# Attention scores as 64-row matmuls, one per head, in place of one full-height matmul over zero-masked keys

## The chip, the core and the metric

The kernel runs on one NeuronCore of one Trainium2 chip. The metric is the device time of one execution in microseconds (us). The engines go by the names of the profile: PE is TensorE's matmul, PEld its weight load, DVE is VectorE, ACT ScalarE, POOL GpSimd, SP SyncE, whose queue issues nearly all DMAs.

## What is computed

One inference step of a four-part decoder trunk: attention, MLP, state-space mixer, MLP, for 512 prompt tokens and 8 sampled tokens. The change lies in the attention of the prompt. There are three groups of window and dilation, (128, 1), (512, 4) and (2048, 16), each with 16 heads of 64 features. Queries and keys are rotated (rope: the two halves of 32 features of a head are mixed by cos and sin), and each query attends to a band of keys:

```python
def dilated_band_attention(q, k, v, dil, nstep):       # q, k, v: (1, 512, 16, 64)
    qb, kx, vx = blocks(q), with_prev(blocks(k)), with_prev(blocks(v))
    scores = jnp.einsum('brnqhe,brnkhe->brnhqk', qb, kx) * SCALE
    scores = jnp.where(mask[None, None, :, None], scores, -jnp.inf)
    mx = jnp.max(scores, -1, keepdims=True)
    p = jnp.exp(scores - mx)
    den = jnp.sum(p, -1)
    o = jnp.einsum('brnhqk,brnkhe->brnqhe', p, vx) / jnp.swapaxes(den, -1, -2)[..., None]
    lse = jnp.swapaxes(mx[..., 0] + jnp.log(den), -1, -2)
```

The three groups' outputs are merged by a softmax over `lse`, and the keys and values of the last positions are outputs too.

## The kernel before

Activations lie features first: a tile of 128 partitions holds 128 features of all 520 tokens. A large product is made of three matmuls for each piece of 128 input features (high part of the weight by high and low part of the activation, low part of the weight by the high part), 24 in a row, for half of the tokens; `dense` issues them (line 249, output `psd`). The kernel is written as a sequence of **slots**. A slot issues one `dense`, then lets each of several **lanes** (generators that hold the small work) take a step, then hands on the weight pipeline (`feed`: `whi` on ACT, lines 186 and 190, and `wlo` on DVE, line 197), evacuates `psd`, and lets the lanes take another step. `after(n, f)` runs `f` at the start of the small work of the n-th next slot. Nothing reorders this afterwards: each engine runs its instructions in the order in which they were written.

The attention runs over 8 chunks `c` of 128 features, that is, of two heads, and in a chunk over the groups g = 0, 1, 2. A group has four slots of q and k (`project_qk`) and two of v (`project_v`); in the last chunk the v slots come after all others. The q and k weights are laid out so that one `psd` holds the first halves of both heads' q and k, and another the second halves. The rope on DVE (lines 575 to 587) gives the tiles F1 and F2. In the slot after, `gather` (lines 594 to 597) has ACT move quarters between partitions in three copies, so that F1 holds q and F2, renamed K, holds k, in rows of half, head, feature. One slot later `heads` (line 604) writes `Kz`: two copies of K, each multiplied by a column of zeros and ones that leaves one head's rows; for g = 1 and 2 it also brings the keys in the order of the dilation, by reading every fourth token.

`attn_scores` (lane A) transposes k for the cache (`kT`, `nT`), then makes the scores: at line 780 the queries of a block are the stationary operand and the keys of both heads in `Kz` the moving one, so that one matmul gives head 0's scores and head 1's scores beside each other in one PSUM bank. Group 0 has four such steps of one block each, groups 1 and 2 two steps of two blocks. After each step DVE adds the mask and takes the maximum (line 792, output `prob`), and ACT takes the exponentials (`exps`, line 807). When group 2 of a chunk is done, `attn_apply` (lane B) merges the groups' factors (`fac`), scales the probabilities (ACT line 846, DVE line 848), transposes them (`pT`, line 869; each bank of them is copied to SBUF by ACT and DVE in turn, lines 256 and 258) and multiplies by V (`oN`, `oR`, line 862, in tiles of 64 columns). `attn_sample` (lane C) does the 8 sampled tokens: `sT` (line 904) is transposed, `spr` (ACT, line 910) takes its exponential, DVE scales that (lines 913 and 914), and `sP` (line 920) transposes it back. `attn_values` transposes v (`vT`, line 666).

PSUM has eight banks: three for `psd`, three (tag S) shared by `kT`, `nT`, `s`, `sT`, `sP`, `pT`, `vT` and others, and two for `oN` and `oR`. A bank that is taken again waits until its last reader is done. The v slots' `psd` is evacuated by ACT (line 618), the q and k slots' by DVE.

Of the kernel before, what the change touches and what calls it, by code (L numbers as in the profile page):

```python
# [11 lines left out]
AF = mybir.ActivationFunctionType  # L12
# [5 lines left out]
P = 128  # L18
D = 1024
KD = D // P  # L20
SEQ = 512
NB = 8
NT = SEQ + NB
# [12 lines left out]
NDB, NSB, NVB = 3, 3, 2  # L36
# [43 lines left out]
class Net:  # L80
# [93 lines left out]
    def split_hi(self, s):  # L174
        nc = self.nc
        for _ in range(2 if s.kind == "qk" else 1):
            s.out.append((self.unit("whi", F32R)[:, 0:D], self.unit("wlo", F32R)[:, 0:D]))
        todo = []
        if s.kind == "qk":
            for ab in range(2):  # L180
                hi, lo = s.out[ab]
                for i, raw in enumerate(s.raw):
                    src = raw.rearrange("p (k h a e) -> p k h a e", k=KD, h=2, a=2)[:, :, :, ab, :]
                    dh = hi.rearrange("p (k i h e) -> p k i h e", k=KD, i=2, h=2)[:, :, i]
                    dl = lo.rearrange("p (k i h e) -> p k i h e", k=KD, i=2, h=2)[:, :, i]
                    nc.scalar.activation(out=dh, in_=src, func=AF.Copy)
                    todo.append((dl, src, dh))
        else:
            hi, lo = s.out[0]
            nc.scalar.activation(out=hi, in_=s.raw[0], func=AF.Copy)  # L190
            todo.append((lo, s.raw[0], hi))
        self.half_split = (s, todo)
# [368 lines left out]
    def project_qk(self, g, x, cur, sqk):  # L561

        nc = self.nc
        F1, F2 = self.pair("F")
        if g != 1:
            cur["K2"] = list(self.pair("K"))
        K = cur["K2"].pop(0)
        cur["F1"][g], cur["F2"][g] = F1, K
        m = {}

        def rope_a(half):
            def f(p1):
                c0 = half * HALF
                m[half] = self.unit("ropem").rearrange("p (i t) -> p i t", i=4)
                nc.vector.tensor_tensor(out=m[half][:, 0:2], in0=p1.unsqueeze(1).broadcast_to((P, 2, HALF)),  # L575
                                        in1=self.cossin[:, :, c0:c0 + HALF], op=ALU.mult)
            return f

        def rope_b(half):
            def f(p2):  # L580
                c0 = half * HALF
                cs = slice(c0, c0 + HALF)
                t = m[half]
                nc.vector.tensor_tensor(out=t[:, 2:4], in0=p2.unsqueeze(1).broadcast_to((P, 2, HALF)),
                                        in1=self.cossin[:, :, cs], op=ALU.mult)
                nc.vector.tensor_tensor(out=F1[:, cs], in0=t[:, 0], in1=t[:, 3], op=ALU.subtract)
                nc.vector.tensor_tensor(out=F2[:, cs], in0=t[:, 2], in1=t[:, 1], op=ALU.add)
                if half:
                    self.after(1, gather)
                    self.after(2, heads)  # L590
            return f

        def gather():
            lo, hi = slice(0, 64), slice(64, P)
            nc.scalar.activation(out=K[lo], in_=F1[hi], func=AF.Copy)
            nc.scalar.activation(out=K[hi], in_=F2[hi], func=AF.Copy)
            nc.scalar.activation(out=F1[hi], in_=F2[lo], func=AF.Copy)

        def heads():
            kz = self.unit("Kz")[:, 0:2 * SEQ].rearrange("p (h t) -> p h t", h=2)  # L600
            src = K[:, 0:SEQ] if g == 0 else K[:, 0:SEQ].rearrange("p (m r) -> p r m", r=4)
            for h in range(2):
                dst = kz[:, h] if g == 0 else kz[:, h].rearrange("p (r m) -> p r m", r=4)
                nc.scalar.activation(out=dst, in_=src, func=AF.Copy, scale=self.hmask[:, h:h + 1])
            cur["Kz"][g] = kz

        for half in range(2):
            self.slot(lambda: self.dense(self.weights(sqk, 0), x, half), rope_a(half))
            self.slot(lambda: self.dense(self.weights(sqk, 1), x, half), rope_b(half))
# [74 lines left out]
    def attn_scores(self, c, g, cur, o, late):  # L684

        nc = self.nc
        F1, F2 = cur["F1"][g], cur["F2"][g]
        kb = self.blocks(F2, g)
        out = self.O[2 + g][0, 0].rearrange("t k (c h) e -> t k c (h e)", h=2)[:, :, c, :]
        self.load_cache(c, g, 0, cur)  # L690
        if not late:
# [2 lines left out]
            yield  # L694
            yield
        bk = self.bank("S", "kT", NSB)
        natural = lambda t: t.rearrange("p (h a e) -> p a h e", h=2, a=2)
        ident = self.ident.rearrange("p (a h e) -> p a h e", a=2, h=2)
        for i in ((3,) if g == 0 else range(4)):
            nc.tensor.transpose(natural(bk[:, i * P:(i + 1) * P]), kb[i], ident)  # L700
        ts = [F1, F2] if late else [F1, F2, cur["V"][g]]
        bn = self.bank("S", "nT", NSB)
        for i, t in enumerate(ts):
            row = bn[0:NB, i * P:(i + 1) * P]
            if i < 2:
                nc.tensor.transpose(natural(row), t[:, SEQ:NT], ident)
            else:
                nc.tensor.transpose(row, t[:, SEQ:NT], self.ident)
        yield
        if g == 0:  # L710
            cur["scr"] = self.dp.tile([3, 3, NB, P], F32, name="newscr", tag="newscr", bufs=2)
# [46 lines left out]

        st = cur["st"]
        neg = self.sp.tile([P, 2, 4], F32, name="neg", tag="neg", bufs=2)  # L760
        kz = cur["Kz"][g]
        both = lambda t: t.rearrange("p (h k) -> p h k", h=2)
        pts = []
        for js in ((0,), (1,), (2,), (3,)) if g == 0 else ((0, 1), (2, 3)):
            if not pts:
                pts = list(self.pair("prob"))
            pt = pts.pop(0)
            b = self.bank("S", "s", NSB)
            tiles, q0 = [], 0
            for j in js:  # L770
                if g == 0:
                    n = P if j == 0 else 2 * P
                    k0 = max(j - 1, 0) * P
                    q, ks = F1[:, j * P:(j + 1) * P], slice(k0, k0 + n)
                    mask = self.m0[:, 2 * P - n:2 * P]
                else:
                    n = P
                    q, ks = F1[:, j:SEQ:4], slice(j * P, (j + 1) * P)
                    mask = self.m0[:, P:2 * P] if g == 1 else self.m2
                nc.tensor.matmul(both(b[:, q0:q0 + 2 * n]), q, kz[:, :, ks], start=True, stop=True)  # L780
                for h in range(2):
                    cs = slice(q0, q0 + n)
                    tiles.append((b[:, cs], pt[:, cs], mask, st[:, 1 if g else 0, j, h, g], neg[:, h, j:j + 1]))
                    for i in range(n // P):
                        key = j if g else j - (n // P - 1) + i
                        cur["P"][g, h, j, key] = pt[:, q0 + i * P:q0 + (i + 1) * P]
                    q0 += n
            a, j1 = 1 if g else 0, js[-1] + 1
            mx, ng = st[:, a, js[0]:j1, :, g, 0], neg[:, :, js[0]:j1].rearrange("p h j -> p j h")
            yield  # L790
            for sc, pr, mask, one, _ in tiles:
                nc.vector.tensor_tensor_reduce(out=pr, in0=sc, in1=mask, scale=1.0, scalar=NEG,  # L792
                                               op0=ALU.add, op1=ALU.max, accum_out=one[:, 0:1])
            nc.vector.tensor_scalar(out=ng, in0=mx, scalar1=-SCALE, scalar2=None, op0=ALU.mult)  # L794
            self.after(1, lambda tiles=tiles: self.exps(tiles))
            yield
# [838 lines left out]
```

## Time and profile before

| | |
|---|---|
| median of 3 runs | 1977.77 us (1975.17 to 1977.83) |
| profiled execution | 1976.72 us, of which 1974.9 us are the span of its instructions |
| PE busy | 1908.9 us, 97% of the span |
| PEld busy | 1853.0 us, 94% |
| DVE busy | 1289.4 us, 65% |
| ACT busy | 954.4 us, 48% |
| mean granted TensorE clock | 0.978 |

Busy times are unions: overlapping matmuls count once. The attention takes the first 660 us of the span. A row of a timeline gives the start and the length of an instruction or of a run of like ones; a matmul's length includes the time in which it fills and drains, so the pace of PE is read from one start to the next. A float32 matmul that isn't a transpose shows as two records, one for each of its two passes.

### The profile page before, as it was taken

To read this page: it belongs to the slowest core of one execution; us is meant where nothing else is said; L and a number is where in the kernel's file an instruction comes from. 1 tells how busy PE (TensorE), PEld (TensorE's weight loads), DVE (VectorE), ACT (ScalarE), POOL (GpSimd) and SP (SyncE) were. 2 spreads that over 40 slices of the span, in tenths; PEclk is the share of its full clock that TensorE was granted. 3 is DMA by queue.
4 is the path that set the end of the run, shared out by engine and by line. 5 is a ranking of instruction groups with operands and counts; after the bars stand their busy time and mean duration, and the time that the engine had idled before them with its cause. 6 is when DMAs were issued, how large, how long until landed. Compare 5 with 4: busy or idle time off the path is not lost.

```text
span 1974.9 us, 38305 instructions
## 1 busy us (share of the span) xinstructions
PE 1908.9 (97%) x15530; PEld 1853.0 (94%) x15530; DVE 1289.4 (65%) x2769; ACT 954.4 (48%) x2085; POOL 73.4 (4%) x92
## 2 busy tenths in 40 slices
PE   7999999999998899999999999998999899999997
PEld 7999999999997899999999999998999899999996
DVE  4676776776788753333337769987889786465435
ACT  4565664664674363525153556634555273525241
POOL 0010010010010000000000000000000000000002
PEclk9999999999998989999999999988999899999999
DMA  6665655555567327655554256644657569987411
GB/s 195 176 181 154 181 157 154 166 157 159 141 206 238 107 98 245 208 170 183 193 186 134 87 175 203 217 133 156 215 186 238 163 184 312 277 277 208 129 33 44
DMA packets 407833, 346.91 MB, mean 176 GB/s; under 512 B 17676, under 2 KB 392932, under 8 KB 405984
## 3 DMA queue, kind: packets, MB, share of 16 engines
q1 hardware_dynamic: 405608, 344.26, 56.3%
q8 instruction: 122, 2.00, 0.4%
q0 software_dynamic: 2048, 0.20, 0.2%
q14 instruction: 55, 0.45, 0.1%
HBM read 322.41 MB, written 130.99 MB: 230 GB/s over the span
## 4 chain that ended last, share of the span: by engine, by line
PE 80%; DVE 14%; ACT 3%; DMA 1%; issue 1%; SPq 0%; POOL 0%; DVEq 0%; ACTq 0%
PE psd L249 68%; PE s L780 3%; DVE wlo L197 2%; DVE conv L1088 2%; PE pT L869 1%; PE oR L862 1%; DVE acc L388 1%; PE oN L862 1%; PE so L945 1%; DVE conv L1216 1%; PE vT L666 1%; ACT ab L1288 1%; DVE ys L1390 1%; PE kT L700 1%; DVE x L392 1%
## 5 line engine op out<-in xcount | busy, mean ns | idle before, releaser
L249 PE MATMUL psd<-x,whi 128*128 128x260 f32 x5920 | 1120.5, 290 | 13.4 <-ACT x L390 5.8
L249 PEld LDWEIGHTS psd<-x,whi 128*128 128x128 f32 x5920 | 930.4, 191 | 33.7 <-issue 15.8
L249 PE MATMUL psd<-x,wlo 128*128 128x260 f32 x2960 | 842.6, 285 | 2.9 <-DVE wlo L197 2.9
L249 PEld LDWEIGHTS psd<-x,wlo 128*128 128x128 f32 x2960 | 563.8, 190 | 3.4 <-DVE wlo L197 3.4
L197 DVE TENSOR_TENSOR wlo<-wraw,whi 128x1024 fp32r<-128x1024 f32 (+1 forms) x321 | 334.2, 1060 | 60.9 <-ACT whi L190 32.3
L249 PE MATMUL psd<-hid,whi 128*128 128x260 f32 (+2 forms) x2048 | 369.8, 283 | 0.1
L190 ACT ACTIVATE whi<-wraw 128x1024 fp32r<-128x1024 f32 x225 | 234.0, 1049 | 211.7 <-PE psd L249 140.9
L249 PEld LDWEIGHTS psd<-hid,whi 128*128 128x128 f32 x2048 | 315.7, 188 | 0.3 <-DVE hid L541 0.3
L249 PE MATMUL psd<-hid,wlo 128*128 128x260 f32 (+2 forms) x1024 | 289.1, 282 | 0.0
L249 PEld LDWEIGHTS psd<-hid,wlo 128*128 128x128 f32 x1024 | 192.7, 188 | 0.0
L489 DVE TENSOR_TENSOR acc<-acc,psd 128x260 f32<-128x260 f32 (+2 forms) x160 | 67.6, 423 | 148.1 <-PE psd L249 148.0
L541 DVE TENSOR_TENSOR hid<-relu,hid 128x260 fp32r<-128x260 f32 x128 | 54.4, 428 | 165.2 <-ACT hid L538 165.2
L534 ACT ACTIVATE relu<-psd 128x260 f32<-128x260 f32 x128 | 49.4, 386 | 159.9 <-PE psd L249 159.1
L807 ACT ACTIVATE prob<-prob,neg 128x128 f32<-128x128 f32 (+1 forms) x192 | 79.5, 416 | 54.1 <-DVE neg L794 53.7
L249 PE MATMUL psd<-ypart,whi 128*128 128x260 f32 x512 | 101.6, 297 | 2.5 <-DVE ypart L1453 2.4
L249 PEld LDWEIGHTS psd<-ypart,whi 128*128 128x128 f32 x512 | 82.6, 197 | 4.2 <-DVE ypart L1453 3.0
L575 DVE TENSOR_TENSOR ropem<-psd,trig 128x520 f32<-128x520 f32 x48 | 33.4, 696 | 77.7 <-PE psd L249 77.6
L1088 DVE SCALAR_TENSOR_TENSOR conv<-raw,cvcols,conv 128x511 f32<-128x511 f32 (+2 forms) x96 | 71.9, 749 | 6.2 <-ACT conv L1083 4.0
L249 PE MATMUL psd<-ypart,wlo 128*128 128x260 f32 x256 | 74.3, 290 | 0.0
L780 PE MATMUL s<-Kz,F 128*128 128x256 f32 (+1 forms) x192 | 71.7, 483 | 0.0
L1170 ACT ACTIVATE raw<-psd 128x260 f32<-128x260 f32 x64 | 24.4, 382 | 84.0 <-PE psd L249 82.4
L792 DVE CUSTOM_DVE_ANT_0 prob<-s,cb 128x128 f32<-128x128 f32 (+1 forms) x192 | 51.6, 318 | 20.5 <-PE s L780 20.5
(252 smaller groups left out, 2277.3 us busy)
## 6 DMA issues: line engine op xcount, KB each, us to landing
wraw<-in_mlp_w_dram SPq DMA_DIRECT2D x128, 512.0 KB
wraw<-in_attn_w_in_dram SPq DMA_DIRECT2D x72, 512.0 KB
wraw<-in_ssm_w_in_dram SPq DMA_DIRECT2D x49, 512.0 KB
cache<-in_cache_kv_w_dram SPq DMA_DIRECT2D x32, 512.0 KB
state<-in_state_ssm_dram SPq DMA_DIRECT2D x32, 512.0 KB
out_dram<-in_cache_kv_w_dram SPq DMA_DIRECT2D x16, 1016.0 KB
qb<-newscr SPq DMA_DIRECT2D x16, 512.0 KB
ab<-acs SPq DMA_DIRECT2D x16, 512.0 KB
```

What stands on the lines that cost most here:

```text
L190: nc.scalar.activation(out=hi, in_=s.raw[0], func=AF.Copy)
L197: self.nc.vector.tensor_tensor(out=lo, in0=src, in1=hi.bitcast(F32), op=ALU.subtract)
L249: self.nc.tensor.matmul(out, a, b[:, cs], start=n == 0, stop=n == 3 * len(w) - 1)
L489: nc.vector.tensor_tensor(out=a, in0=a, in1=ps, op=ALU.add)
L534: nc.scalar.activation(out=t[:, 0], in_=ps, func=AF.Relu)
L541: nc.vector.tensor_tensor(out=h[m][1][:, cs], in0=t[:, 1], in1=h[m][0][:, cs].bitcast(F32), op=ALU.subtract)
L575: nc.vector.tensor_tensor(out=m[half][:, 0:2], in0=p1.unsqueeze(1).broadcast_to((P, 2, HALF)), in1=self.cossin[:, :, c0:c0 + HALF], op=ALU ...
L780: nc.tensor.matmul(both(b[:, q0:q0 + 2 * n]), q, kz[:, :, ks], start=True, stop=True)
L792: nc.vector.tensor_tensor_reduce(out=pr, in0=sc, in1=mask, scale=1.0, scalar=NEG, op0=ALU.add, op1=ALU.max, accum_out=one[:, 0:1])
L807: self.nc.scalar.activation(out=pr, in_=pr, func=AF.Exp, scale=SCALE, bias=ng, accum_out=st[:, 1:2])
L862: nc.tensor.matmul(bank[hs, j * P:(j + 1) * P], vt[:, hs], pr, start=first, stop=last)
L1088: nc.vector.scalar_tensor_tensor(out=t[:, j:SEQ], in0=raw[:, 0:SEQ - j], scalar=w[:, 3 - j:4 - j], in1=t[:, j:SEQ], op0=ALU.mult, op1=ALU.add)
```

## The change

The weights are laid out with the head outermost, so that F1 and F2 come out in rows of head, (q or k), feature. `gather` now makes K in rows of head, half, feature, in six copies of 32 partitions; for g = 1 and 2 it also brings the keys in the order of the dilation, so that each of the four K copies becomes one of 512 tokens, read with a step of four, and one of the 8 sampled tokens. `heads` and `Kz` are gone. The transposes for the cache need no permuted identity, and for g = 1 and 2 read k without a step. The scores are two matmuls, each with the 64 rows of one head as contraction, head 0 on partitions 0 to 63 and head 1 on 64 to 127, each into a bank of its own; group 0 has two steps of two blocks, groups 1 and 2 one step of four blocks.

```diff
         def gather():
-            lo, hi = slice(0, 64), slice(64, P)
-            nc.scalar.activation(out=K[lo], in_=F1[hi], func=AF.Copy)
-            nc.scalar.activation(out=K[hi], in_=F2[hi], func=AF.Copy)
-            nc.scalar.activation(out=F1[hi], in_=F2[lo], func=AF.Copy)
-
-        def heads():
-            kz = self.unit("Kz")[:, 0:2 * SEQ].rearrange("p (h t) -> p h t", h=2)
-            src = K[:, 0:SEQ] if g == 0 else K[:, 0:SEQ].rearrange("p (m r) -> p r m", r=4)
             for h in range(2):
-                dst = kz[:, h] if g == 0 else kz[:, h].rearrange("p (r m) -> p r m", r=4)
-                nc.scalar.activation(out=dst, in_=src, func=AF.Copy, scale=self.hmask[:, h:h + 1])
-            cur["Kz"][g] = kz
+                a, b = slice(64 * h, 64 * h + 32), slice(64 * h + 32, 64 * h + 64)
+                for d, s in ((a, F1[b]), (b, F2[b])):
+                    if g == 0:
+                        nc.scalar.activation(out=K[d], in_=s, func=AF.Copy)
+                    else:
+                        nc.scalar.activation(out=K[d, 0:SEQ].rearrange("p (r m) -> p r m", r=4),
+                                             in_=s[:, 0:SEQ].rearrange("p (m r) -> p r m", r=4), func=AF.Copy)
+                        nc.scalar.activation(out=K[d, SEQ:NT], in_=s[:, SEQ:NT], func=AF.Copy)
+                nc.scalar.activation(out=F1[b], in_=F2[a], func=AF.Copy)
...
-        for js in ((0,), (1,), (2,), (3,)) if g == 0 else ((0, 1), (2, 3)):
...
-            b = self.bank("S", "s", NSB)
+        for js in ((0, 1), (2, 3)) if g == 0 else (range(4),):
+            pts = self.pair("prob")
+            bs = [self.bank("S", "s", NSB) for _ in range(2)]
...
-                nc.tensor.matmul(both(b[:, q0:q0 + 2 * n]), q, kz[:, :, ks], start=True, stop=True)
+                cs = slice(q0, q0 + n)
                 for h in range(2):
-                    cs = slice(q0, q0 + n)
+                    hs, b, pt = slice(64 * h, 64 * h + 64), bs[h], pts[h]
+                    nc.tensor.matmul(b[:, cs], q[hs], F2[hs, ks], start=True, stop=True)
```

The change also moves instructions. On ACT, in the v slots of group 1 of each of the chunks 1 to 6, the order before is this; `K` and `F` are the last two of gather's three copies, `spr` the sampled tokens' exponential, `prob` by line 807 an exponential of scores and by line 846 the scaling.

```order
L596 ACTIVATE K<-F 64x520
L597 ACTIVATE F<-F 64x520
L910 ACTIVATE spr,sm<-sT,sm 16x323
L190 ACTIVATE whi<-wraw 128x1024
L618 ACTIVATE V<-psd 128x260
L846 ACTIVATE prob<-prob,fac 128x128 x4
L604 ACTIVATE Kz<-K,cb 128x512 x2
L807 ACTIVATE prob,st<-prob,neg 128x256 x2
L618 ACTIVATE V<-psd 128x260
L807 ACTIVATE prob,st<-prob,neg 128x256 x2
L186 ACTIVATE whi<-wraw 128x8x64 x4
L256 ACTIVATE pT<-pT 128x512
```

The same place in the changed kernel: the rows begin with the second half of the ten copies of `gather`; ahead of them, and not shown, stand four scalings (`prob`, now line 834), four exponentials (line 795) and the first five copies.

```order
L599 ACTIVATE K<-F 32x512
L601 ACTIVATE K<-F 32x8
L599 ACTIVATE K<-F 32x512
L601 ACTIVATE K<-F 32x8
L602 ACTIVATE F<-F 32x520
L898 ACTIVATE spr,sm<-sT,sm 16x323
L190 ACTIVATE whi<-wraw 128x1024
L615 ACTIVATE V<-psd 128x260
L795 ACTIVATE prob,st<-prob,neg 128x256 x4
L615 ACTIVATE V<-psd 128x260
L256 ACTIVATE pT<-pT 128x512
L834 ACTIVATE prob<-prob,fac 128x128 x3
```

Moved: the four scalings stand ahead of `gather`, no longer behind it, and all copies that replace `Kz` stand ahead of `spr`; the four `whi` stand behind the copy of `pT`.

On PE, in the next group's q and k slots of the same chunk, the order before is this; `pT` are the transposed probabilities, `psd` the rows of `dense`. The first bank of `pT` has been taken just there, and `vT` comes one slot later.

```order
L249 MATMUL psd<-x,wlo 128x260
L869 MATMUL pT<-cb,prob 128x128 x4
L920 MATMUL sP<-cb,spr 128x16 x2
L920 MATMUL sP<-cb,spr 67x16
L249 MATMUL psd<-x,whi 128x260 x2
```

And that next slot's end, still of the kernel before:

```order
L249 MATMUL psd<-x,wlo 128x260
L869 MATMUL pT<-cb,prob 128x128 x4
L666 MATMUL vT<-cb,V 128x128 x4
L249 MATMUL psd<-x,whi 128x260 x2
L249 MATMUL psd<-x,wlo 128x260
```

In the changed kernel the second bank of `pT`, `sP` and `vT` stand together, after the group's first `dense`; the first bank of `pT` stands one slot ahead of them.

```order
L249 MATMUL psd<-x,wlo 128x260
L857 MATMUL pT<-cb,prob 128x128 x4
L908 MATMUL sP<-cb,spr 128x16 x2
L908 MATMUL sP<-cb,spr 67x16
L663 MATMUL vT<-cb,V 128x128 x4
L249 MATMUL psd<-x,whi 128x260 x2
```

Moved: `vT` and both banks of `pT` are one slot earlier; `sP` stays behind the same `dense`. In both kernels `vT` takes the bank that the first `pT` had, and so waits for ACT's copy of it.

## Rows read from the trace of the kernel before

**Rows 1.** The page's chain of work that ended last, by engine.

```profile
PE 80%; DVE 14%; ACT 3%; DMA 1%; issue 1%; SPq 0%; POOL 0%; DVEq 0%; ACTq 0%
```

**Rows 2.** Windows: PE, PEld, DVE, ACT, POOL busy (instructions), granted clock, DMA.

```profile
45.00:560.00 515.00, 515.00 (x4098) 484.61 (x4097) 361.61 (x964) 295.77 (x767) 39.27 (x56) 0.99 0.59 167
...
600.90:602.40 1.50, 0.00 (x0) 0.00 (x0) 1.50 (x3) 0.23 (x1) 0.00 (x0) 1.00 1.89 720
603.20:606.70 3.50, 3.50 (x18) 3.33 (x19) 3.50 (x5) 2.15 (x3) 0.00 (x0) 0.51 0.09 28
...
688.60:695.40 6.80, 5.64 (x24) 5.34 (x25) 4.54 (x10) 5.34 (x11) 0.00 (x0) 0.50 0.52 180
```

**Rows 3.** Timeline of PE, chunk 4, groups 0 to 2: start, length, records.

```profile
336.27 0.59 PE L780 MATMUL s<-Kz,F 128*128 128x256 f32 x2
...
339.59 0.44 PE L904 MATMUL sT<-cb,ss 128*16 128x128 f32 x3
...
343.66 1.02 PE L780 MATMUL s<-Kz,F 128*128 128x512 f32 x2
...
344.76 0.28 PE L249 MATMUL psd<-x,wlo 128*128 128x260 f32 x1
...
347.40 1.02 PE L780 MATMUL s<-Kz,F 128*128 128x512 f32 x2
...
355.37 0.65 PE L666 MATMUL vT<-cb,V 128*128 128x128 f32 x4
```

**Rows 4.** Timeline of ACT, the same stretch of chunk 4.

```profile
342.91 0.64 ACT L595 ACTIVATE K<-F 64x520 f32<-64x520 f32 x1
...
344.89 0.52 ACT L910 ACTIVATE spr<-sT,sm 16x323 f32<-16x323 f32 x1
...
345.41 1.05 ACT L190 ACTIVATE whi<-wraw 128x1024 fp32r<-128x1024 f32 x1
346.37 0.36 ACT L618 ACTIVATE V<-psd 128x260 f32<-128x260 f32 x1
346.63 1.26 ACT L846 ACTIVATE prob<-prob,fac 128x128 f32<-128x128 f32 x4
347.80 2.33 ACT L604 ACTIVATE Kz<-K,cb 128x512 f32<-128x512 f32 x2
350.03 0.49 ACT L807 ACTIVATE prob<-prob,neg 128x256 f32<-128x256 f32 x1
...
351.02 0.36 ACT L618 ACTIVATE V<-psd 128x260 f32<-128x260 f32 x1
...
354.35 0.57 ACT L256 ACTIVATE pT<-pT 128x512 f32<-128x512 f32 x1
```

**Rows 5.** Timeline of PE, products in two column tiles of 64, chunk 3.

```profile
302.15 0.66 PE L862 MATMUL oR<-pT,Vt 128*64 128x128 f32 x8
302.73 0.75 PE L666 MATMUL vT<-cb,V 128*128 128x128 f32 x4
```

**Rows 6.** Weight loads of the score line: ns shortest/median/longest.

```profile
L780 PEld LDWEIGHTS s<-Kz,F x192: 187/320/337, 48.7 to 615.2; 128*128 128x128 f32 x192
```

**Rows 7.** Timeline of PE, a score step of group 1 in chunk 1.

```profile
139.70 1.31 PE L780 MATMUL s<-Kz,F 128*128 128x256 f32 x4
...
141.09 0.28 PE L249 MATMUL psd<-x,wlo 128*128 128x260 f32 x1
```

**Rows 8.** The copies to Kz on ACT: ns shortest/median/longest.

```profile
L604 ACT ACTIVATE Kz<-K,cb x48: 708/1206/1239, 38.5 to 579.9; 128x512 f32<-128x512 f32 x48
```

**Rows 9.** Timeline of DVE, the same stretch of chunk 4.

```profile
339.79 0.70 DVE L584 TENSOR_TENSOR ropem<-psd,trig 128x520 f32<-128x520 f32 x1 [1.78 <-PE psd L249]
...
340.87 0.42 DVE L587 TENSOR_TENSOR F<-ropem 128x260 f32<-128x260 f32 x1
...
343.01 0.20 DVE L828 TENSOR_TENSOR den<-fac,st 128x48 f32<-128x48 f32 x1
...
343.78 0.21 DVE L831 TENSOR_TENSOR fac<-fac,facm 128x48 f32<-128x48 f32 x1
```

More of the change, by code (lines that the diff above doesn't have):

```diff
@@ L183, in split_hi @@
                     src = raw.rearrange("p (k h a e) -> p k h a e", k=KD, h=2, a=2)[:, :, :, ab, :]
-                    dh = hi.rearrange("p (k i h e) -> p k i h e", k=KD, i=2, h=2)[:, :, i]
-                    dl = lo.rearrange("p (k i h e) -> p k i h e", k=KD, i=2, h=2)[:, :, i]
+                    dh = hi.rearrange("p (k h i e) -> p k i h e", k=KD, i=2, h=2)[:, :, i]
+                    dl = lo.rearrange("p (k h i e) -> p k i h e", k=KD, i=2, h=2)[:, :, i]
                     nc.scalar.activation(out=dh, in_=src, func=AF.Copy)
@@ L589, in f @@
                     self.after(1, gather)
-                    self.after(2, heads)
             return f
         def gather():
-            lo, hi = slice(0, 64), slice(64, P)
-            nc.scalar.activation(out=K[lo], in_=F1[hi], func=AF.Copy)
-            nc.scalar.activation(out=K[hi], in_=F2[hi], func=AF.Copy)
-            nc.scalar.activation(out=F1[hi], in_=F2[lo], func=AF.Copy)
-        def heads():
-            kz = self.unit("Kz")[:, 0:2 * SEQ].rearrange("p (h t) -> p h t", h=2)
-            src = K[:, 0:SEQ] if g == 0 else K[:, 0:SEQ].rearrange("p (m r) -> p r m", r=4)
-            for h in range(2):
-                dst = kz[:, h] if g == 0 else kz[:, h].rearrange("p (r m) -> p r m", r=4)
-                nc.scalar.activation(out=dst, in_=src, func=AF.Copy, scale=self.hmask[:, h:h + 1])
-            cur["Kz"][g] = kz
+            for h in range(2):
+                a, b = slice(64 * h, 64 * h + 32), slice(64 * h + 32, 64 * h + 64)
[7 more added lines that the diff above has]
+                nc.scalar.activation(out=F1[b], in_=F2[a], func=AF.Copy)
         for half in range(2):
@@ L687, in attn_scores @@
         F1, F2 = cur["F1"][g], cur["F2"][g]
-        kb = self.blocks(F2, g)
+        kb = [F2[:, i * P:(i + 1) * P] for i in range(4)]
         out = self.O[2 + g][0, 0].rearrange("t k (c h) e -> t k c (h e)", h=2)[:, :, c, :]
@@ L696, in attn_scores @@
         bk = self.bank("S", "kT", NSB)
-        natural = lambda t: t.rearrange("p (h a e) -> p a h e", h=2, a=2)
-        ident = self.ident.rearrange("p (a h e) -> p a h e", a=2, h=2)
         for i in ((3,) if g == 0 else range(4)):
-            nc.tensor.transpose(natural(bk[:, i * P:(i + 1) * P]), kb[i], ident)
+            nc.tensor.transpose(bk[:, i * P:(i + 1) * P], kb[i], self.ident)
         ts = [F1, F2] if late else [F1, F2, cur["V"][g]]
@@ L704, in attn_scores @@
             row = bn[0:NB, i * P:(i + 1) * P]
[L705 to L708, printed above, removed]
+            nc.tensor.transpose(row, t[:, SEQ:NT], self.ident)
         yield
@@ L760, in attn_scores @@
         neg = self.sp.tile([P, 2, 4], F32, name="neg", tag="neg", bufs=2)
-        kz = cur["Kz"][g]
-        both = lambda t: t.rearrange("p (h k) -> p h k", h=2)
-        pts = []
-        for js in ((0,), (1,), (2,), (3,)) if g == 0 else ((0, 1), (2, 3)):
-            if not pts:
-                pts = list(self.pair("prob"))
-            pt = pts.pop(0)
-            b = self.bank("S", "s", NSB)
+        for js in ((0, 1), (2, 3)) if g == 0 else (range(4),):
+            pts = self.pair("prob")
+            bs = [self.bank("S", "s", NSB) for _ in range(2)]
             tiles, q0 = [], 0
@@ L786, in attn_scores @@
                         cur["P"][g, h, j, key] = pt[:, q0 + i * P:q0 + (i + 1) * P]
-                    q0 += n
+                q0 += n
             a, j1 = 1 if g else 0, js[-1] + 1
```

## The prediction, made before the changed kernel had run

> **What bounds the kernel now.** I read the chain of waits first: PE holds 80% of it [rows 1]. Then the windows: from 45 to 560 us, nearly the whole attention, PE is busy in 515.00 of 515.00 us, at a clock of 0.99, while ACT has 295.77 and DVE 361.61 [rows 2]. So in this stage the sum of what PE issues is the time, as long as nobody makes it wait. The last view is the timelines of the three engines over one chunk, because an engine that is 57% busy can still be late at one place: the place to look at is 355.37, where PE transposes v [rows 3]. Its bank was last read by ACT's copy of `pT`, which began at 354.35 and took 0.57 [rows 4]. PE came 0.45 us after that copy had ended. That is the whole margin, and the change moves both sides of it.
>
> **The change on PE.** Group 0 first. A step with 512 columns begins at 343.66, and the third matmul of the `dense` behind it at 344.76; less two matmuls of 0.12 that is 0.86 us. From 343.66 to the next step at 347.40 it is 3.74, so a `dense` of 24 takes 2.88 [rows 3]. The three steps of 512 columns and one of 256 (half: 0.43) make 3.0 us a chunk. In the changed kernel each head streams half of these columns. If the two heads run side by side, group 0 streams 1.5 us. No row shows two row tiles at work. The nearest are the column tiles of [rows 5]: eight records of 128 columns, which at the pace above (0.43 a record of 256) would stream 0.86, are over in 0.58. Paired they stream 0.43, and 0.15 is left for the change of tiling. I add 0.1 for going in and 0.1 for coming out, and take 0.35 an excursion. Group 0 has two: the step of blocks 0 and 1 costs 0.64 + 0.35 = 0.99, that of blocks 2 and 3 0.85 + 0.35 = 1.20, together 2.19 for 3.0: **0.8 us less a chunk, 6.6 us in eight.**
>
> Groups 1 and 2 take their queries with a step of four tokens, and there the load sets the pace: 320 ns for the median, 187 for the quick ones [rows 6]. A step of four passes costs 141.09 - 139.70 - 0.24 = 1.15 us [rows 7], two steps 2.3 a group. The changed kernel has sixteen half-height passes in eight pairs, so again eight times the load, plus one more change of tiling: 2.3 to 2.6. I count nothing gained there; the transposes that now read k without a step give back about what the change of tiling takes. Below, if loads of the two heads queue, is a rival.
>
> The Trainium skill bears on this in "TensorE: Matmul & The Clock Gate", section "LDWEIGHTS (loading the stationary operand)": a load's time goes by its columns, and a load of few rows takes as long as one of all rows. By it the halves of the height save nothing, and only running side by side can pay for loading twice as often; the trace shows loads of one height alone, so no row here tests it.
>
> **The change on ACT.** Removed: three gather copies at (344.89 - 342.91) / 3 = 0.66 us and, two at a time, the Kz copies: 350.03 - 347.80 = 2.23 with a step of four [rows 4]. Added for groups 1 and 2: four copies with a step of four, four of 8 tokens, two plain ones of 0.66. A copy costs by its length, not its partitions, in lack of a row for fewer. The stepped reading adds 0.5 us (708 against 1206 ns for one and the same shape [rows 8]), so 0.66 + 0.5, about 1.15. For 8 tokens the nearest row is a copy of 260 in 0.26 [rows 4]; between nothing and that I take 0.15. Together **G = 4.6 + 0.6 + 1.3 = 6.5 us a group**, with 5.5 (copies that overlap) and 7.2 (that don't) as bounds. Now it is 4.2 in two slots.
>
> **Where this falls on the path.** Take T = 336.27, group 0's first score step. `vT` came at T + 19.10 [rows 3]. PE's work ahead of it changes: two steps of 0.86 gone, the first step 0.43 to 0.99, the second 0.86 to 1.20, and one `dense` of 2.88 less, since `vT` stands a slot earlier. So PE would come at 19.10 - 1.72 + 0.56 + 0.34 - 2.88 = **T + 15.4**.
>
> ACT's queue at that place begins with four scalings that wait for DVE's last `fac`. The last q and k `dense` of group 1 ends at 0.99 + 2.88 = 3.87; the rope starts 0.20 later (339.79 against 339.59 [rows 3, 9]), takes 1.50 to the end of F2, and `den` to `fac` 0.98 [rows 9]: T + 6.55. Then in order: scalings 1.17 (346.63 to 347.80), four exponentials 1.8 (two of 256 columns 0.99, two of 128 a little less), G 6.5, `spr` 0.52, `whi` 0.96, V 0.26, four exponentials 2.0, V 0.26, `pT` 0.57 [rows 4]. That is 14.0, so the copy ends at **T + 20.6**. `sP` waits on the same queue (`spr` ends at 16.5, DVE scales it) but is through by then. PE waits 20.6 - 15.4 = **5.2 us**, with G's bounds 4.2 to 5.9. It happens in chunks 1 to 6, which have these orders; chunk 0 has no `attn_apply` beside it, and in chunk 7 `vT` comes later. Six times 5.2 is **31 us**.
>
> Behind the late copy on ACT stand the next `whi`, on which DVE's `wlo` waits, and behind that the rope of group 2. Their buffers have two slots of room, and a stalled PE gives them more, so I add nothing. What is late next, if G is above its price, is the copy of V in group 2, which stands behind eight exponentials and another G.
>
> **The clock.** After PE stood still from 600.90 to 602.40, the clock was granted at 0.51 (the level of 1.2 GHz) for 3.50 us of work, in which half, 1.7 us, is lost; around 689 it was 0.50 over 5.64 us of work, 2.8 lost [rows 2]. So a wait of 5 us may cost 0 to 2.8 more. I take 1.7, the nearer row, six times: **10 us**.
>
> **The sum**, against the profiled execution's own 1976.72 us (1 us below the median, 1.8 above its span): 1976.7 - 6.6 + 31 + 10 = **2011 us**. With the bounds of this case (waits 25 to 35, clock 0 to 17) 1995 to 2022.
>
> **The rivals.** *The copies are hidden (faster).* ACT is idle for 43% of the stage, and if it is through at T + 15.4, PE's 6.6 us are gained: 1970. For this ACT's 14.0 us must shrink to 8.8: G at 1.3, a fifth of its price, or much of the rest begun earlier than the orders let it. 15 in 100. *The heads don't run side by side, or their loads queue (slower still).* Queued loads alone: groups 1 and 2 have sixteen loads where eight took 2.3 us, so 2 us more each, 32 us in eight chunks, on top of the waits: 2043. Wholly one after the other, group 0 also streams its 3.0 us plus 0.7, a loss of 0.7 a chunk for the gain of 0.8, and PE comes to `vT` 1.5 us later, so the wait is 3.7: 1976.7 + 6 + 32 + 22 + 10 = 2047. The column tiles of [rows 5] speak against both, for tiles that share their rows. 13 in 100. *The waits are small (about no change).* If the wait is about 1 us and the clock stays up, 6 us of waits eat the 6.6 us: 1976. 7 in 100. *The forecast*, with its bounds: 65 in 100.
>
> **The numbers.** A difference under 0.2% (4 us) is about what a measurement of this kernel can't tell from none. The range leaves out the faster rival below and the far end of the slowest above: 1984 to 2040. Faster 0.17, same 0.07, slower 0.76.
>
> **What would show it.** Right: in chunks 1 to 6 an idle time of PE before `sP` and `vT`, released by ACT's `pT` and by `spr`, and a lower clock behind it; `gather` in a block of 6 to 7 us on ACT; scores of group 0 at 1.0 and 1.2 us an excursion. Wrong: `vT` with no wait (then the time is below 1980), or score records of the two heads that don't start in pairs (then above 2035). It is wrong in size if the small copies or the stepped ones cost much less than 0.15 and 1.15.

## The result, and the profile of the changed kernel

The changed kernel took 2027.82 us (median of 4 runs, 2023.48 to 2029.53) against 1977.64 for the kernel before: a ratio of 1.0256, interval 1.0243 to 1.027. The profiled execution took 2028.2, its span is 2026.4, 51.5 more than before.

The chain of waits of the changed kernel by engine, which answers to [rows 1]:

```profile
PE 69%; DVE 15%; ACT 11%; issue 2%; DMA 2%; SPq 0%; POOL 0%; ACTq 0%; DVEq 0%
```

PE's share has fallen from 80% to 69, ACT's has risen from 3% to 11. The windows, with the columns of [rows 2]: first the same stretch as there, then the stretch from the first matmul of a `dense` to the 3,901st, which holds the attention; the last two are the stretches of low clock behind the waits of chunks 1 and 4.

```profile
45.00:560.00 515.00, 481.32 (x3907) 453.76 (x3907) 327.02 (x874) 299.20 (x774) 36.41 (x52) 0.95 0.54 154
13.15:748.68 735.53, 682.42 (x5459) 640.65 (x5459) 485.21 (x1241) 415.74 (x1060) 46.02 (x65) 0.95 0.55 157
131.70:138.50 6.80, 4.37 (x20) 4.37 (x21) 6.26 (x13) 5.82 (x18) 1.38 (x2) 0.50 0.02 1
...
377.40:384.20 6.80, 5.65 (x26) 5.65 (x27) 4.98 (x9) 4.53 (x12) 1.04 (x2) 0.50 0.16 40
```

The stretch of the same 3,900 matmuls in the kernel before:

```profile
13.67:698.33 684.66, 671.13 (x5267) 628.51 (x5267) 492.21 (x1273) 380.99 (x972) 46.03 (x65) 0.98 0.58 168
```

From 45 to 560 us PE was busy without a gap before; now it stands still for 33.7 us of it. The second row of the changed kernel and the row of before carry a balance. Idle time is the stretch less PE's busy time. The clock's loss is half of PE's busy time in those windows that were granted 0.50. The rest is work at full clock.

| us, same 3,900 matmuls | before | changed | difference | forecast |
|---|---|---|---|---|
| PE idle | 13.5 | 53.1 | +39.6 | +31 |
| lost to the half clock | 15.2 | 32.3 | +17.1 | +10 |
| PE's work at full clock | 655.9 | 650.2 | -5.7 | -6.6 |
| stretch | 684.7 | 735.5 | +50.9 | +34 |

What lies outside that stretch, ahead of it and behind it, differs by 0.6 us. Where PE waits is told by the view of waits (us in total, times, longest), from 45 to 680 us:

```profile
PE vT L663 <- ACT pT L256: 17.5, 6, 2.9
PE sP L908 <- DVE spr L902: 12.5, 6, 2.1
PE vT L663 <- ACT V L615: 5.1, 8, 1.5
PE s L770 <- DVE Kt L714: 3.6, 2, 2.0
PE pT L857 <- ACT spr L898: 1.7, 1, 1.7
```

The first two rows are six times each, once in each of the chunks 1 to 6: 30.0 us, 5.0 a chunk. Chunk 4 on PE, with T = 358.17 (answers to [rows 3]):

```profile
358.17 0.93 PE L770 MATMUL s<-K,F 64*128 64x128 f32 x8
359.02 0.50 PE L249 MATMUL psd<-x,whi 128*128 128x260 f32 x2
...
362.00 0.44 PE L892 MATMUL sT<-cb,ss 128*16 128x128 f32 x3
362.37 1.13 PE L770 MATMUL s<-K,F 64*128 64x256 f32 x8
...
375.31 0.33 PE L908 MATMUL sP<-cb,spr 16*128 16x16 f32 x3 [2.09 <-DVE spr L902]
378.55 1.13 PE L663 MATMUL vT<-cb,V 128*128 128x128 f32 x4 [2.91 <-ACT pT L256]
379.33 0.78 PE L249 MATMUL psd<-x,whi 128*128 128x260 f32 x2
...
384.50 0.49 PE L857 MATMUL pT<-cb,prob 128*128 128x128 f32 x3
...
390.22 2.14 PE L770 MATMUL s<-K,F 64*128 64x128 f32 x16
```

The `dense` from 359.02 takes 2.98 us to `sT`; the one from 379.33, right behind the two waits, takes 5.17 to `pT`. The 2.2 us between them are the half clock. The same chunk on ACT (answers to [rows 4]):

```profile
364.62 1.28 ACT L834 ACTIVATE prob<-prob,fac 128x128 f32<-128x128 f32 x4 [4.80 <-DVE fac L819]
...
367.69 1.12 ACT L599 ACTIVATE K<-F 32x512 f32<-32x512 f32 x1
368.71 0.19 ACT L601 ACTIVATE K<-F 32x8 f32<-32x8 f32 x1
...
373.30 0.63 ACT L602 ACTIVATE F<-F 32x520 f32<-32x520 f32 x1
373.96 0.52 ACT L898 ACTIVATE spr<-sT,sm 16x323 f32<-16x323 f32 x1
...
377.93 0.57 ACT L256 ACTIVATE pT<-pT 128x512 f32<-128x512 f32 x1
```

`gather` holds ACT from 367.69 to 373.93, 6.24 us (forecast 6.5). `spr` and the copy of `pT` stand behind it, and the copy ends at T + 20.3 (forecast 20.6).

### The profile page after: what moved, and what is told of

The parts are those of the page before. It is cut to its first block, busy times and chain, and to the rows that moved or that the text cites. A ratio compares the mean times of both kernels' runs of the same rounds, so it can differ in the third digit from the quotient of the medians.

```text
span 2026.4 us, 38670 instructions
## 1 busy us (share of the span) xinstructions
PE 1920.7 (95%) x15722; PEld 1865.5 (92%) x15722; DVE 1282.5 (63%) x2737; ACT 988.9 (49%) x2173; POOL 73.8 (4%) x92
## 4 chain that ended last, share of the span: by engine, by line
PE 69%; DVE 15%; ACT 11%; issue 2%; DMA 2%; SPq 0%; POOL 0%; ACTq 0%; DVEq 0%
PE psd L249 59%; ACT K L599 3%; ACT prob L795 3%; DVE wlo L197 2%; PE s L770 2%; DVE conv L1076 1%; ACT F L602 1%; PE vT L663 1%; DMA wraw<-in_ssm_w_out_dram 1%; ACT whi L190 1%; DVE acc L388 1%; PE so L933 1%; ACT prob L834 1%; DVE conv L1204 1%; DVE ys L1378 1%
## 5 line engine op out<-in xcount | busy, mean ns | idle before, releaser
L249 PEld LDWEIGHTS psd<-x,wlo 128*128 128x128 f32 x2960 | 570.6, 193 | 3.2 <-DVE wlo L197 3.2
L599 ACT ACTIVATE K<-F 32x512 f32<-32x512 f32 x64 | 72.0, 1124 | 4.3 <-DVE F L586 3.1
L538 ACT ACTIVATE hid<-relu 128x260 fp32r<-128x260 f32 x128 | 53.5, 418 | 9.2 <-PE psd L249 6.1
```

The source lines that it names most:

```text
L249: self.nc.tensor.matmul(out, a, b[:, cs], start=n == 0, stop=n == 3 * len(w) - 1)
L538: nc.scalar.activation(out=h[m][0][:, cs], in_=t[:, 1], func=AF.Copy)
L599: nc.scalar.activation(out=K[d, 0:SEQ].rearrange("p (r m) -> p r m", r=4), in_=s[:, 0:SEQ].rearrange("p (m r) -> p r m", r=4), func=AF.Copy)
```

## The experiments

**Theory.** ACT's block of copies stands ahead of `spr` and of the first `pT`'s copy; PE pays for every microsecond of it beyond a small margin, and then at half clock. **Rivals:** the wait comes from the order in which PSUM's banks are taken (`vT` and both `pT` a slot earlier), whatever ACT does; or the two heads don't overlap, and the scores eat the time. Each time stands beside runs of the kernel before on the same chip, whose medians were 1974.5 to 1975.2.

**e1_pool**: the copies of `gather` on POOL.

```diff
-                        nc.scalar.activation(out=K[d], in_=s, func=AF.Copy)
+                        nc.gpsimd.tensor_copy(out=K[d], in_=s)
...
-                nc.scalar.activation(out=F1[b], in_=F2[a], func=AF.Copy)
+                nc.gpsimd.tensor_copy(out=F1[b], in_=F2[a])
```

> All of the changed kernel's gather copies are issued on POOL, which is busy 4% of the span, instead of ACT; all else stays. Theory (the block of 6.2 us of copies on ACT ahead of the first pT copy makes PE wait 5.0 us in each of chunks 1 to 6, and each wait is followed by a half clock that costs 2.2 to 2.9): ACT reaches the pT copy about 6 us earlier, before PE comes to vT, so both waits go, and with them the lost clock: 2027.8 - 30 - 15 + 3 (the two drops that the kernel before has too) - 3 (the smaller waits behind V in chunk 0) = about 1983, range 1972 to 1992. Rival 1 (the order of the PSUM banks, vT and both pT a slot earlier, makes the wait, whatever ACT has to do): the two waits stay, above 2015. Rival 2 (POOL's copies are slow or hold up DVE, so that K comes late at kT): waits at kT in place of those at vT, 1995 or more.

Measured: 1974.16 us, ratio 1.0003 (0.9989 to 1.0016). `sP` and `vT` wait no more in any chunk, and from 45 to 560 us no half clock is left. The order of the banks is untouched, so that rival falls. The kernel only draws level with the one before, though PE has less work. What shows beside it is that DVE's work on the same tiles takes longer with the copies on POOL. DVE's rows of the changed kernel (count, busy us, mean ns):

```profile
L836 DVE TENSOR_SCALAR prob<-prob,fac 128x128 f32<-128x128 f32 x120 | 26.2, 280 | 0.3
L927 DVE TENSOR_TENSOR cache<-cache 67x1024 f32<-67x1024 f32 x8 | 9.7, 1214 | 0.0
```

and of e1_pool, with POOL's copy:

```profile
L836 DVE TENSOR_SCALAR prob<-prob,fac 128x128 f32<-128x128 f32 x120 | 47.1, 456 | 0.3
L927 DVE TENSOR_TENSOR cache<-cache 67x1024 f32<-67x1024 f32 x8 | 14.7, 1840 | 0.0
...
L599 POOL COPY K<-F 32x512 f32<-32x512 f32 x64 | 86.4, 1349 | 205.6 <-DVE F L586 186.7 <-ACT prob L834 16.5
```

One and the same scaling takes 456 ns in the mean for 280. Its median hardly moves (281 ns for 279); the longest takes 1230, so some of the 120 are held up for most of the length of a copy. The Trainium skill says in "SBUF — State Buffer", section "SBUF: two separate sides", that VectorE (in a two-port mode, or with two inputs in SBUF) and GpSimd share a pair of ports, which one of them holds for a whole instruction while the other is blocked; these rows agree with it, though no run tests the ports alone. PE's work at full clock is 653.7 us here, 3.5 more than in the changed kernel; whether the slower DVE alone makes that is not separated.

**e2_plain**: six plain copies in every group; the score matmuls read the keys with the step.

```diff
-                    q, ks = F1[:, j:SEQ:4], slice(j * P, (j + 1) * P)
+                    q, ks = F1[:, j:SEQ:4], slice(j, SEQ, 4)
```

> The copies of gather take no dilated order in groups 1 and 2: six plain copies of 520 tokens in every group, and the score matmuls read the keys with a step of four instead (kT reads them so too, as before). Theory: gather falls from 6.2 to about 3.8 us, so the waits of 5.0 us in chunks 1 to 6 fall to about 2.6, some 14 us less, and the clock still falls behind them: 2013 if the stepped keys cost PE nothing, up to 2035 if each of the 16 stepped passes takes twice as long. What decides is the idle time of PE at sP and vT, 2.4 to 2.8 us a chunk. Rival (bank order): idle time there stays 5.0.

Measured: 2004.84 us, ratio 1.0146 (1.0131 to 1.0161). The waits and one copy:

```profile
PE vT L658 <- ACT pT L256: 16.2, 6, 2.7
...
L596 ACT ACTIVATE K<-F 32x520 f32<-32x520 f32 x96 | 61.1, 636 | 10.0 <-DVE F L586 8.1
```

`gather` is 6.24 - 6 x 0.64 = 2.4 us shorter, and the wait 2.3 (5.0 to 2.7). The half clock behind it now lasts 3.4 us instead of 6.8 and costs 1.7. The stepped keys cost PE 0.1 us a score step (2.26 for 2.17). The total is 8 us below the forecast range, which had left the half clock as it was: in the stretch 26.2 us are lost to it, for 32.3, and the waits behind V (5.1 us) are gone too.

**e3_double**: each stepped copy is made twice.

```diff
-                        nc.scalar.activation(out=K[d, 0:SEQ].rearrange("p (r m) -> p r m", r=4),
+                        for _ in range(2):
+                            nc.scalar.activation(out=K[d, 0:SEQ].rearrange("p (r m) -> p r m", r=4),
```

> Each of the four stepped copies of gather (groups 1 and 2) is made twice, so gather takes 6.2 + 4.5 = 10.7 us on ACT; nothing else differs. Theory: the idle time of PE at sP and vT in chunks 1 to 6 grows by the same 4.5 us, from 5.0 to 9.5, 27 us; the margin of 0.7 us of group 2's vT behind V is used up as well, up to 3.8 a chunk in seven chunks: between 2055 and 2085. Rival (bank order): the idle time stays 5.0 a chunk and the time is within 5 us of 2028.

Measured: 2113.37 us, ratio 1.07 (1.0681 to 1.072).

```profile
PE vT L664 <- ACT V L616: 41.9, 8, 6.0
PE sP L909 <- DVE spr L903: 39.3, 6, 6.6
PE vT L664 <- ACT pT L256: 16.6, 6, 2.8
```

At `sP` and `vT` behind `pT` it is now 9.3 a chunk, 4.3 more for 4.5 us of copies. The total passed the forecast range because the wait behind V came eight times with 4.8 to 6.0 us, where seven of up to 3.8 were forecast, and because each new wait took its half clock (50.2 us lost in the stretch, 32.3 before the edit).

**e6_late**: all of `gather` two slots later, behind the copy of `pT`.

```diff
-                    self.after(1, gather)
+                    self.after(1 if cur["late"] else 3, gather)
```

> All of gather stands on ACT as in the changed kernel, but two slots later (in the first slot of the next group, behind the copy of the first pT bank), save in the last chunk. Theory: the queue ahead of the pT copy is 6.2 us shorter, it ends before PE comes to vT, and the idle time at sP and vT goes with its clock drops; K is then ready about when kT wants it (estimated 0.6 us after it), and the weights that ACT rounds behind gather come 4 us later: 1983 plus up to 0.6 us in each of 14 groups, 1978 to 1998. Rival (bank order): 2015 or more, waits at vT unchanged. Rival 2 (the work of ACT is only moved and blocks the next thing): waits of 2 us or more at kT or at psd behind wlo, above 2000.

Measured: 2018.21 us, ratio 1.0223 (1.0206 to 1.024). The waits at `sP` and `vT` are gone, and another of 4.1 us is there:

```profile
PE kT L695 <- ACT Vt L668: 20.5, 5, 4.1
PE pT L857 <- ACT Vt L668: 4.9, 1, 4.9
```

The time is 20 us above the forecast range, and the second rival came true. Not `K` was late, as forecast (0.6 us), but the next bank: `kT` takes the one that `vT` had, and ACT's copy of `vT` stands behind `gather` and the four `whi`. ACT's block is paid at both of the places tried.

**e4_serial** and **e13_serial_lines**: all matmuls of head 0 in a step, then all of head 1; the second has them on two lines.

```diff
-                    nc.tensor.matmul(b[:, cs], q[hs], F2[hs, ks], start=True, stop=True)
+                    mm[h].append((b[:, cs], q[hs], F2[hs, ks]))
...
+            for x, y, z in mm[0] + mm[1]:
+                nc.tensor.matmul(x, y, z, start=True, stop=True)
```

> The score matmuls of a step are issued in another order: all of head 0, then all of head 1, no longer by turns, so that neighbours use the same 64 rows; nothing else differs from the changed kernel. It prices the running side by side. Theory (the two heads overlap fully when they alternate, and not in this order): a step of groups 1 and 2 takes 16 passes at 0.23 us instead of 8, 4.0 us for 2.17; group 0's two steps 1.6 and 2.05 us for 0.96 and 1.17: 5.2 us a chunk, 42 us in eight, less 1.5 us of each of the six waits at sP and vT, since PE comes later: about 2060, 2045 to 2070. Rival (the passes overlap in any order, or the pace is set by something both orders share): within 5 us of 2028.

> The same program as e4_serial, with the matmuls of head 0 and those of head 1 on two source lines, so that the trace tells them apart. In e4_serial a score step of groups 1 and 2 took 3.2 us and not the 4.0 of two heads one after the other. Theory (a matmul starts ahead of earlier ones of the other head, since it uses other rows): records of head 1 begin about 1.0 us after the step's first, while half of head 0's eight records are still to come. Rival (matmuls start in the order of the program, and only the pace is faster): head 1's first record begins behind head 0's eighth, later than 1.7 us into the step. The time is that of e4_serial, 2040 to 2050, in either case.

Measured: 2045.72 us (ratio 1.0361, 1.0339 to 1.0383) and 2050.1 (one run). In the changed kernel the heads overlap: eight pairs of passes take 2.17 us, where eight passes took 2.3 before. In this order a step of groups 1 and 2 takes 3.2 us at the full clock, but not 4.0, and group 0 nothing more. PE's work in the stretch of e4_serial grew by 15 us, not 42, the loss to the half clock by 7.6 (39.8 us), and the waits at `sP` and `vT` stayed 5.0 a chunk. A step of group 1 in e13_serial_lines, line 777 head 0, line 779 head 1:

```profile
235.92 1.43 PE L777 MATMUL s<-K,F 64*128 64x128 f32 x5
236.96 0.50 PE L779 MATMUL s<-K,F 64*128 64x128 f32 x1
237.19 0.39 PE L777 MATMUL s<-K,F 64*128 64x128 f32 x1
237.29 0.40 PE L779 MATMUL s<-K,F 64*128 64x128 f32 x1
...
237.65 0.39 PE L777 MATMUL s<-K,F 64*128 64x128 f32 x1
237.76 1.33 PE L779 MATMUL s<-K,F 64*128 64x128 f32 x5
```

Head 1's first record begins 1.04 us into the step, with three of head 0's eight still to come: TensorE runs one head's matmul ahead of earlier ones of the other. So the theory of e13 holds, with three records still to come where four were forecast, and that of e4 was wrong in size.

**e12_before_twice**: the kernel before, in group 1 both copies to `Kz` made twice.

```diff
-            for h in range(2):
+            for h in ((0, 1, 0, 1) if g == 1 else (0, 1)):
```

> The kernel before with one edit: in group 1 the two copies to Kz are made twice, 2.3 us more on ACT ahead of the copy of the first pT bank; nothing else differs. Theory: the margin of 0.45 us read from the rows of before is used up and PE waits 2.3 - 0.45 = 1.9 us at vT in each of the chunks 1 to 6, 11 us, with up to 1.7 us of clock behind each: 1974.5 + 11 + 0 to 10 = 1986 to 1996. Rival (ACT's queue has more room there than the rows say, so the wait of the changed kernel has another cause): within 4 us of the kernel before.

Measured: 1984.62 us, ratio 1.0051 (1.0037 to 1.0066).

```profile
PE vT L666 <- ACT pT L256: 9.7, 6, 1.7
```

The same wait at the same six places, 1.6 us each for 2.3 of copies: the margin is 0.7, where 0.45 was read. No half clock came behind these six waits, so the time ended 1.4 us under the range.

**e7_dma**, **e8_rope_dma**, **e9_rope_act**: three ways to take the copies off ACT's path. e7 makes them DMAs on SP's queue and has the stepped keys of e2_plain.

```diff
-                        nc.scalar.activation(out=K[d], in_=s, func=AF.Copy)
+                    nc.sync.dma_start(out=K[d], in_=s)
```

In e8 the rope also writes groups 1 and 2 in the order of the dilation, so that neither queries nor keys need a step; its core:

```diff
+                    dst = F[:, 0:SEQ].rearrange("p (r m) -> p m r", r=4)[:, c0 // 4:(c0 + n) // 4]
+                    nc.vector.tensor_tensor(out=dst, in0=row(t[:, i]), in1=row(t[:, j]), op=op)
...
-                    q, ks = F1[:, j:SEQ:4], slice(j * P, (j + 1) * P)
+                    q, ks = F1[:, j * P:(j + 1) * P], slice(j * P, (j + 1) * P)
```

e9 is e8 with the copies on ACT, head 1's two slots later.

```diff
-                    self.after(1, gather)
+                    self.after(1, lambda: gather((0,)))
+                    self.after(1 if cur["late"] else 3, lambda: gather((1,)))
```

> Gather's six plain copies are DMAs on SP's queue instead of ACT instructions, in every group; the score matmuls and kT of groups 1 and 2 read the keys with a step of four, as in e2_plain. Theory: no copy stands on ACT ahead of the pT copy and none on POOL beside DVE, so no wait at sP and vT and no slowed DVE: PE's work as in e2_plain (653 us up to the end of the attention's products for 656 before), clock drops as in e1_pool: about 1969, 1960 to 1978. Rival 1 (SP's queue stands still until the rope is done, so that weights land late): PE waits at psd behind whi, above 1985. Rival 2 (K lands late): waits at kT, above 1980.

> As e7_dma, and the rope on DVE writes F1 and F2 of groups 1 and 2 in the order of the dilation (a step of 128 elements in its output, one small instruction more for the 8 sampled tokens), so that queries and keys are both read without a step. Theory: a score step of groups 1 and 2 then runs at group 0's pace, 8 pairs of 0.105 us and 0.35 for the change of tiling, 1.2 us for 2.2: 2.0 us a chunk, 16 us in eight, on top of e7_dma: about 1953, 1943 to 1965. Rival 1 (the load doesn't set the pace there): as e7_dma. Rival 2 (DVE's stepped output takes twice as long or more and makes F late): less gain, waits at s behind DVE, 1960 to 1985.

> As e8_rope_dma, but the six plain copies stay on ACT: head 0's three one slot after the rope as in the changed kernel, head 1's three two slots later, behind the first pT copy (in the last chunk all at once). Theory: 1.9 us of copies are left ahead of the pT copy for 6.2, so PE's wait of 5.0 falls to about 0.8 in chunks 1 to 6; the 1.9 us behind it are fewer than the 6.2 that made PE wait 4.1 at kT in e6_late, so none there; PE's work as in e8_rope_dma, and the last chunk's waits as in the changed kernel: about 1970, 1958 to 1982. Rival (any copy on ACT is paid by PE): 23 us of copies in six chunks stay on the path, above 1990.

Measured: 2003.4 us (ratio 1.0154, 1.0134 to 1.0175), 1990.75 (1.009, 1.0074 to 1.0106) and 1980.83 (1.0034, 1.0019 to 1.0049), e7 and e8 beyond their forecast ranges, e9 at the end of its own. In e7 the waits at `vT` are gone; DVE's waits and PE's tell the rest:

```profile
DVE qb L730 <- DMA qb<-newscr: 32.1, 16, 6.8
...
PE s L765 <- DVE Kt L709: 8.7, 6, 2.4
PE kT L690 <- DMA K<-F: 4.5, 2, 2.9
```

No weight was late, but `qb`, another load on the same SP queue, for which DVE waits nowhere in the changed kernel; its copy of `kT`, further behind in DVE's order, then makes the scores wait. Why `qb` lands late on that queue was not traced. In e8 PE's work was 637.8 us, 18.9 less than e7's 656.7 (forecast 16), but the waits behind `qb` and `kT`'s copy stayed: 13.0 us at the scores. In e9, with 1.9 us of copies at each place, three short waits stay a chunk:

```profile
PE vT L667 <- ACT pT L256: 6.5, 6, 1.1
PE kT L699 <- ACT Vt L672: 4.9, 5, 1.0
PE s L774 <- DVE Kt L718: 3.0, 5, 0.6
```

**e10_rope_pool** and **e11_rope_pool_kt**: the rope of e8 with the six plain copies on POOL; in e11 ACT copies `kT` in groups 1 and 2.

```diff
-            nc.vector.tensor_copy(Kt.rearrange("p i f -> p (i f)"), bk)
+            nc.scalar.activation(out=Kt.rearrange("p i f -> p (i f)"), in_=bk, func=AF.Copy)
```

> The rope writes groups 1 and 2 in the order of the dilation as in e8_rope_dma, and gather's six plain copies are on POOL as in e1_pool, which had them stepped. Theory: PE's work up to the end of the attention's products as in e8_rope_dma plus what e1_pool had more than the changed kernel (638 + 3), idle time and clock drops as in e1_pool (17 and 11), and up to 0.6 us a chunk where a score step waits for the bank that DVE's copy of kT reads, as in e9_rope_act: 1974 - 12 + 5 = about 1965, 1957 to 1972. Rival (POOL's copies slow DVE as much as the stepped ones did, and the shorter scores are eaten by waits behind DVE): 1972 to 1982.

> As e10_rope_pool, and the copy of kT in groups 1 and 2 is on ACT, no longer on DVE. Theory: a score step takes two of the three S banks at once, and the second was kT's, which DVE reads late; ACT is idle for some 8 us at that place, so the waits at s go, with the clock drops behind the longer ones: 3 to 8 us less than e10_rope_pool, 1952 to 1966. Rival (the waits there are DVE's at another place, or ACT's copy comes late too): within 3 us of e10_rope_pool.

Measured: 1957.83 us, ratio 0.9916 (0.9903 to 0.9928), and 1955.46, ratio 0.9904 (0.9889 to 0.9918). Both beat the kernel before and the changed one; whether e11 beats e10 is not settled, since the intervals overlap and the 2.4 us between them lie in the rival's range. The waits at the scores behind `kT`'s copy are gone in e11, but in e10 they were only 1.2 us. The same 3,900 matmuls in e10, the load of its score matmuls (ns shortest/median/longest) and DVE's scaling:

```profile
13.42:678.65 665.23, 648.12 (x5459) 607.38 (x5460) 512.46 (x1273) 288.61 (x852) 173.73 (x209) 0.98 0.60 173
...
L773 PEld LDWEIGHTS s<-K,F x384: 182/188/188, 49.2 to 575.8; 64*128 64x128 f32 x192
...
L839 DVE TENSOR_SCALAR prob<-prob,fac 128x128 f32<-128x128 f32 x120 | 34.5, 348 | 0.3
```

PE is idle for 17.1 us of 665.2, loses 9.7 to the clock and works 638.4. The load is 188 ns where the step of four made it 326, and plain copies on POOL slow the scaling to 348 ns, not 456.

## Why the prediction was right, and where it was off

The direction, the mechanism and the place were right; the time came out 17 us above the point. It lies inside the range only because that had been widened for the rivals: it is 6 us above the 2022 that the forecast's own bounds allowed, since two of its terms were too small.

**PE's work**: right. Group 0's two excursions took 0.96 and 1.17 us (forecast 0.99 and 1.20), a step of groups 1 and 2 2.17 (forecast 2.3), records of the two heads 7 ns apart. The work fell by 5.7 us, for 6.6. The rival of queued loads is refuted. The rule that the prediction drew from the Trainium skill, "TensorE: Matmul & The Clock Gate", section "LDWEIGHTS (loading the stationary operand)", agrees: a load of 64 rows took 182 to 188 ns in e10, as one of 128 rows did at its quickest [rows 6]. The trace of the kernel before could have tested it, against what the prediction says of it: with 128 columns, loads of 16 rows (`sP`) took 135 ns in the mean, those of 128 rows (`pT`) 141. One reading was a slip: 0.43 us is a record of 512 columns, not of 256; the 0.86 worked out there holds.

**The wait**: right. The forecast priced the whole stop at 5.2 us, from PE's coming at T + 15.4 to the end of the copy at T + 20.6, and named `sP` and `vT` as its places without a split; measured are 2.1 at `sP` and 2.9 at `vT`. PE stood before `sP` from T + 15.05, `spr` ended at T + 16.3 (forecast 16.5), and by the copy's end `sP` was through. That ACT's copies cause it is shown from both sides: none on ACT, no wait (e1_pool); 2.4 us less, 2.3 less (e2_plain); 4.5 more, 4.3 more (e3_double); and 2.3 more in the kernel before makes the same wait there (e12_before_twice).

**The clock**: mis-sized. The forecast took 1.7 us from a drop of 3.5 us behind a wait of 1.5 [rows 2]. Behind these waits the half level (1.2 GHz) lasted 6.8 us, with 4.4 to 5.7 us of work in it: 15.2 us for the six, 17.1 net in the stretch, against 10.

**What is late next**: counted as nothing, measured 9.6 us (39.6 less 30.0). At both ends of the attention, for which no wait was forecast, PE did wait: at `vT` for V (5.1 us, 4.0 of them there), which the text had named as next, and in chunk 7 at `pT` for `spr` (1.7) and at the scores for DVE's copy of `kT` (3.6). The first two are gone in e1_pool and e2_plain, so the larger copies did reach PE here. A score step there takes two of three S banks at once, which the text didn't see; that this makes the wait is argued from the order of the banks, and e11, where ACT makes that copy, has no such wait. These two terms, 7 and 9.6, are nearly the whole miss of 17.

**The rivals**: hidden copies would have needed G at a fifth of its price; it was at 0.96 of it.

## What to carry to other kernels

When one engine is busy without a gap, a helper at half load is judged by its queue at the place where the busy engine takes something from it: sum what stands there ahead, compare with the margin, and count what is added in full. Copies that are moved later, or onto another queue, can come back as a wait for the next thing in that queue (`vT`'s copy, `qb`); of the places tried here only the engine that was 4% busy had the room, and it charged DVE for it; the copies on DVE itself were not tried. What paid was to remove the stepped reading at its source, in the rope, and then to move the plain copies.

## What was not expected of the hardware

Matmuls on different 64-row halves started out of program order in e13_serial_lines: up to three records of one head began after the first of the other, though all stand ahead of it. So what is said of the kernel before, that each engine runs its instructions in the order in which they were written, does not hold for these. The Trainium skill says in "TensorE: Matmul & The Clock Gate", section "The mechanism", that matmuls start and end in program order; the rows of e13_serial_lines differ in the starts, and the measurement decides. DVE writing 128x260 with a step of 128 elements took 0.63 us for 0.43 (e8_rope_dma).

Behind the waits the half clock lasted longer where PE had stood longer: none behind 1.6 us (e12_before_twice), 3.4 us behind 2.7 (e2_plain), 6.8 behind 2.1 and 2.9 with 0.33 of work between. That is no rule: a wait of 1.5 us in the kernel before had 3.5 us of half clock behind it [rows 2], and 4.1 us in e6_late had 3.4. Nor does it take a wait. In the kernel before the clock also fell at a place where PE was busy throughout:

```profile
309.60:313.10 3.50, 3.50 (x19) 3.30 (x18) 0.83 (x3) 0.48 (x1) 0.00 (x0) 0.51 1.48 486
```

Just ahead of it PE had run sixteen matmuls of a single column (`so`, 1.95 us from 307.34), and the same stands ahead of the drop at 459.9 and of two in the changed kernel (251.2 and 415.0), though not every such row has a drop behind it.
